# One order for the opening of a convolution module: squares on three engines, sums in pairs, the norm inside one product, loads by three queues

## The chip, the cores and the metric

The kernel runs on one core of a Trainium2 chip. The metric is the device time of one execution in microseconds. Five engines work side by side, each with its own stream of instructions: TensorE (PE in the profile) multiplies matrices into PSUM, VectorE (DVE), ScalarE (ACT) and GpSimd (POOL) do elementwise work, and SyncE (SP) issues most of the loads. ACT and POOL have queues for loads too.

## The reference

Two layers of a decoder trunk on one sequence of 512 positions and 1024 channels, in float32. Layer 0 mixes by a convolution module, layer 1 by sparse attention; after each comes a SwiGLU block. The part that matters here is the opening of layer 0:

```python
def rmsnorm(x, g):
    xf = x.astype(jnp.float32)
    y = xf * lax.rsqrt(jnp.mean(xf * xf, axis=-1, keepdims=True) + RMS_EPS)
    return (y * g.astype(jnp.float32)).astype(x.dtype)

def conformer_conv_module(h, w_in, b_in, w_dw, b_dw, ln_g, ln_b, w_out):
    a, g = jnp.split(h @ w_in + b_in, 2, axis=-1)
    u = a * jax.nn.sigmoid(g)
    u = lax.conv_general_dilated(u, w_dw[:, None, :], ..., feature_group_count=D_MODEL) + b_dw
    ... # layer norm over channels, silu
    return u @ w_out

h = rmsnorm(x, norm_mix[0]); x = x + conformer_conv_module(h, ...)
```

## The kernel before

Everything is kept transposed: channels on the 128 partitions, the 512 positions along the free dimension. `x` is eight tiles x0 to x7. Products are made at nearly float32 precision from halves: each operand is split into a rounded high part and the rest, its low part, and three matmuls (high by high, low by high, high by low) are added in PSUM. ACT writes the high parts, `wh` of a weight unit (L233) and `hh` of an x tile (L327, multiplied by the norm's gain). DVE writes the low parts, `wl` (L242) and `hl` (L328).

Weights come in units. Units 0 to 3 (`cw_s`, 256 KB) hold the columns of the first output tile, two x tiles' rows each. Units 4 to 17 (`cw_in`, 512 KB) hold one output tile each. SP loads them into three buffers `wr`; `wh` and `wl` have two buffers each.

The module's first product has 16 output tiles: A0 to A7 are the values and G0 to G7 the gates of eight groups of 128 channels. A0 and G0 are made in the opening: for each x tile six matmuls, 48 in all (`mm3`, L293 to L295). Then come A1 (unit 4), G1 (unit 5), A2 (unit 6), G2 (unit 7), A3 (unit 8), G3 (unit 9) and so on, 24 matmuls each, made by `proj_tile` (A1 and G1 at L409 to L411, the others at L293 to L295).

The RMS norm's divisor is applied behind the product. The sum of squares over channels starts in `sum_x`: ACT or DVE squares an x tile and DVE adds it into `acc`. `norm_a` (L350) lets TensorE sum `acc` over partitions, and DVE finds the reciprocal root in twelve small instructions. `norm_b` (L361) lets TensorE spread the root over the partitions, and ACT copies it to `R`. `norm_1` calls the one after half of A1, `norm_2` the other after half of G1. From then on `glu` can work: DVE multiplies the gate and the value by R, ACT takes the sigmoid, and DVE writes `u`. DVE then convolves some groups tap by tap (`cv`), POOL others from taps that ACT scales (`pv<-pv,tap`, L546), and TensorE the rest with band matrices (`cpe<-uf,bd`, L593), which POOL loads behind a copy of one column (`held`, L485).

A scheduler orders the instructions of each engine; `tc.keep_in_program_order` fixes the place of those it is called on.

Of the kernel before, what the change touches and what calls it, by code (L numbers as in the profile page):

```python
# [11 lines left out]
F32R = mybir.dt.float32r  # L12
BF16 = mybir.dt.bfloat16
I32 = mybir.dt.int32
AF = mybir.ActivationFunctionType
# [53 lines left out]
NPH = PH_B + 8 * len(PE_CONV)  # L69
WARM0 = 10  # L70
WARMS = {"t": 2, "r": 5}
SUM_V = (0, 3)


QV_ORDER = (0, 1, 2, 3, 4, 5, 6, 7, 8, 9)
# [59 lines left out]
def trunk(ctx: ExitStack, tc: tile.TileContext, A, out):  # L135
# [9 lines left out]
    def nm(s):  # L145
        cnt[0] += 1
        return f"{s}_{cnt[0]}"
# [67 lines left out]
    def parted(ins):  # L215
        return ins if hold[0] == "pe" else held(ins)

    def w_dma(i):
# [4 lines left out]
        raw_dma[i] = parted(after(nc.sync.dma_start(t[:, :cols], ap), state.get("behind")))  # L223
        raws[i] = t

    def w_hi(i):
# [31 lines left out]
    zb = cst.tile([P, P], BF16, name="zb")  # L258
    nc.vector.memset(zb, 0.0)
    dummy = cst.tile([P, 1], F32, name="dummy")  # L260
    nc.scalar.activation(dummy, zb[:, :1], AF.Copy)
    vec = cst.tile([P, NVEC], F32, name="vec")
    nc.sync.dma_start(vec, A["vec"])
    x = [xp.tile([P, T], F32, tag=f"x{m}", name=f"x{m}") for m in range(NK)]
    for m in range(NK):
        nc.sync.dma_start(x[m], A["xT"][m])
        if m in (0, 2, 4):
            w_dma(m // 2)
    cx0 = ExitStack()
    cb = cx0.enter_context(tc.tile_pool(name="cb", bufs=1, side="right"))  # L270
# [10 lines left out]
    def v(col, n=1):  # L281
        return vec[:, col:col + n]
# [37 lines left out]

    hh, hl = [None] * NK, [None] * NK

    def split_x(m, gcol):
        hh[m] = hps[0].tile([P, T], F32R, tag=f"hh{m}", name=nm(f"hh{m}"))
        hl[m] = hps[0].tile([P, T], F32R, tag=f"hl{m}", name=nm(f"hl{m}"))
        g = v(gcol + m)
        parted(nc.scalar.activation(hh[m], x[m], AF.Copy, scale=g))  # L327
        parted(nc.vector.scalar_tensor_tensor(hl[m], x[m], g, hh[m], ALU.mult, ALU.subtract))  # L328

    def sum_x(m, acc, eng=None, on_v=False):  # L330
        sq = acc if m == 0 else tp.tile([P, T], F32, tag="sq", name=nm("sq"))
        if on_v:
            nc.vector.tensor_tensor(sq, x[m], x[m], ALU.mult)
        else:
            parted(nc.scalar.activation(sq, x[m], AF.Square))
        if m > 0:
            parted((eng or nc.gpsimd).tensor_tensor(acc, acc, sq, ALU.add))

# [59 lines left out]
                    hooks[k]()  # L398
        return pss

    def proj_tile(pool, tag, xh=None, xl=None, mid=None, fixed=False):
        xh, xl = xh or hh, xl or hl
        ps = pool.tile([P, T], F32, tag=tag, name=nm("pp"))
        wh, wl = next_w()
        for k in range(NK):
            c = slice(k * P, (k + 1) * P)
            if fixed:
                kept = tc.keep_in_program_order
                kept(nc.tensor.matmul(ps, wh[:, c], xh[k], start=k == 0, stop=False))  # L409
                kept(nc.tensor.matmul(ps, wh[:, c], xl[k], start=False, stop=False))  # L410
                kept(nc.tensor.matmul(ps, wl[:, c], xh[k], start=False, stop=k == NK - 1))  # L411
            else:
                mm3(ps, wh[:, c], wl[:, c], xh[k], xl[k], k == 0, k == NK - 1)
            if k == 3:
                w_lo()
                if mid:
                    mid()
        return ps


# [23 lines left out]


    def conv_module():
        acc = new_acc()
        with ExitStack() as cx:
            cp = cx.enter_context(tc.tile_pool(name="cp", bufs=1, side="right"))
            ct = cx.enter_context(tc.tile_pool(name="ct", bufs=2, side="right"))  # L450
# [20 lines left out]


            pend = [pm.tile([P, T], F32, tag="pm", name=nm("pp")) for _ in range(2)]
            for k in range(NK):
                split_x(k, V_NM0)
                if k % 2 == 0:
                    wh, wl = next_w()
                if k == 0:
                    load_tables()
                for m in range(2):  # L480
                    c = slice(k % 2 * 256 + m * P, k % 2 * 256 + (m + 1) * P)
                    mm3(pend[m], wh[:, c], wl[:, c], hh[k], hl[k], k == 0, k == NK - 1)
                sum_x(k, acc, nc.vector, k in SUM_V)
            held = ct.tile([P, 1], F32, name="held", bufs=1)
            tc.keep_in_program_order(nc.gpsimd.tensor_copy(held, hl[NK - 1][:, :1]))  # L485
            for n in range(BAND_BUFS):
# [3 lines left out]

            def norm_1():
                last["r"] = norm_a(acc, pa, "pa")

            def glu(i, pA, pG):
                gr = ct.tile([P, T], F32, tag="A", bufs=3, name=f"gr{i}")
# [249 lines left out]
                        conv_pe(PE_CONV.index(c), c, ups[c])  # L745

            for i in range(1, NK):
                pA = proj_tile(pm, "pm", mid=norm_1 if i == 1 else None, fixed=i == 1)

                def gated():  # L750
                    glu(i - 1, *pend)
                    after_glu(i - 1)

                def norm_2():
                    nonlocal R
                    R = norm_b(last["r"], pa, "pa")
                    gated()
# [1595 lines left out]
```

## Time and profile before

| what | us |
| --- | --- |
| median of 3 runs | 1163.84 |
| lowest and highest | 1162.61, 1164.09 |
| profiled execution | 1163.65 |
| its span, first to last instruction | 1161.9 |
| PE busy | 1149.5 (99%) |
| DVE busy | 950.6 (82%) |
| ACT busy | 642.0 (55%) |
| POOL busy | 312.1 (27%) |

A row of the timeline gives the start in the span, the duration, the engine, the line, the operation, what is written and read, and how many instructions are merged; in brackets stands how long the engine was idle before and what ended that. A row of the windows gives the stretch, the busy time of PE, PE's weight loads, DVE, ACT and POOL, the TensorE clock that was granted, the share of the DMA engines that was busy, and GB/s. A row of the waits gives who waited for whom, for how long in total, how often, and the longest.

### The profile page before, as it was taken

The page shows a single profiled execution, that of the slowest core. Times are in us where ns is not written, and L with a number is a line of the kernel's source. Part 1 is how long each engine was busy: PE and PEld are TensorE (multiplying, and loading weights), DVE is VectorE, ACT ScalarE, POOL GpSimd, SP SyncE. Part 2 cuts the span into 40 slices and gives each one's busy share as a digit, 9 for nine tenths or more (in the row PEclk, how much of TensorE's full clock was granted, in tenths as well). Part 3 has the DMA queues.
Part 4 walks back from the last instruction along what each step waited for, and adds up shares of the span by engine and source line. Part 5 has one row for each costly group of instructions (what it writes and reads, how often), then busy time and mean ns, then how long its engine had stood idle before and what let it go on. Part 6 is the DMA issues. An engine that isn't in the chain of part 4 may idle for free.

```text
span 1161.9 us, 20767 instructions
## 1 busy us (share of the span) xinstructions
PE 1149.5 (99%) x7645; PEld 989.9 (85%) x7645; DVE 950.6 (82%) x1874; ACT 642.0 (55%) x1207; POOL 312.1 (27%) x406
## 2 busy tenths in 40 slices
PE   9999899999999999999999999999999999999998
PEld 6788688899999989998778877778889999998998
DVE  6999798999999878874465888865798999987876
ACT  5665555555555555454344688864355555554443
POOL 2699102011111101210124577860001111110120
PEclk9999999999999999999999999999999999999999
DMA  8633727377777768844455211134326777766892
GB/s 297 280 101 113 203 94 228 109 179 181 192 188 179 178 187 226 180 122 125 135 158 139 80 29 34 31 110 127 109 91 168 189 185 190 188 174 175 222 194 96
DMA packets 81141, 179.69 MB, mean 155 GB/s; under 512 B 29328, under 2 KB 30992, under 8 KB 80016
## 3 DMA queue, kind: packets, MB, share of 16 engines
q1 hardware_dynamic: 56896, 105.26, 28.7%
q0 software_dynamic: 24144, 73.12, 27.9%
q8 instruction: 60, 0.98, 0.3%
q14 instruction: 41, 0.34, 0.1%
HBM read 163.50 MB, written 4.75 MB: 145 GB/s over the span
## 4 chain that ended last, share of the span: by engine, by line
PE 94%; DVE 4%; ACT 1%; issue 1%; DMA 0%; SPq 0%; POOL 0%; ACTq 0%; DVEq 0%
PE st L1000 43%; PE pp L293 8%; PE pp L295 8%; PE pp L294 8%; PE O L2030 3%; PE T L1998 3%; PE st L294 2%; PE st L293 2%; PE st L295 2%; PE cpe L593 2%; PE S L1952 2%; PE pp L411 2%; PE pp L409 2%; PE pp L410 2%; PE pv L1818 1%; PE S L1953 1%
## 5 line engine op out<-in xcount | busy, mean ns | idle before, releaser
L1000 PE MATMUL st<-bo,sh 128*128 128x256 f32 (+1 forms) x1008 | 259.8, 333 | 0.0
L233 ACT ACTIVATE wh<-wr 128x1024 fp32r<-128x1024 f32 (+3 forms) x144 | 148.9, 1035 | 153.5 <-issue 48.3
L242 DVE TENSOR_TENSOR wl<-wr,wh 128x1024 fp32r<-128x1024 f32 (+3 forms) x144 | 176.6, 1226 | 52.4 <-ACT wh L233 48.6
L1000 PE MATMUL st<-bo,sl 128*128 128x256 f32 x720 | 203.3, 282 | 0.0
L1000 PEld LDWEIGHTS st<-bo,sh 128*128 128x128 f32 x1008 | 170.6, 189 | 20.1
L1000 PEld LDWEIGHTS st<-bo,sl 128*128 128x128 f32 x720 | 136.7, 190 | 0.1
L295 PE MATMUL pp<-hh,wl 128*128 128x512 f32 x304 | 120.2, 398 | 2.2 <-DVE wl L242 2.2
L293 PE MATMUL pp<-hh,wh 128*128 128x512 f32 x304 | 120.7, 400 | 0.5 <-ACT hh L327 0.2
L294 PE MATMUL pp<-hl,wh 128*128 128x512 f32 x304 | 119.7, 395 | 0.0
L986 DVE TENSOR_TENSOR sl<-S,sh 128x512 fp32r<-128x512 f32 x144 | 93.1, 687 | 16.9 <-ACT sh L985 16.6
L1000 PE MATMUL st<-bo,wh 128*128 128x256 f32 (+1 forms) x432 | 103.1, 316 | 0.0
L1000 PE MATMUL st<-oz,soh 128*128 128x256 f32 x512 | 88.0, 277 | 0.0
L961 POOL DMA_DIRECT2D S<-fw_x x36 | 21.1, 588 | 235.1 <-ACT c L1015 127.2
L985 ACT ACTIVATE sh<-S 128x512 fp32r<-128x512 f32 x144 | 82.2, 619 | 0.3
L1039 ACT ACTIVATE g<-g 128x512 f32<-128x512 f32 x36 | 22.8, 633 | 106.6 <-DVE g L1036 106.6
L1000 PE MATMUL st<-bo,wl 128*128 128x256 f32 x288 | 80.4, 279 | 0.0
L967 POOL DMA_DIRECT2D S<-fw_x x36 | 42.7, 1185 | 136.7 <-DMA S<-fw_x 131.5
L1000 PEld LDWEIGHTS st<-oz,soh 128*128 128x128 f32 x512 | 77.5, 188 | 0.4
L546 POOL TENSOR_TENSOR pv<-pv,tap 128x512 f32<-128x512 f32 x49 | 71.2, 1454 | 19.7 <-ACT tap L540 16.4
L1000 PEld LDWEIGHTS st<-bo,wh 128*128 128x128 f32 x432 | 70.8, 188 | 6.6
L1986 POOL TENSOR_SCALAR Pm<-Pm,rq,gates 128x512 f32<-128x512 f32 (+2 forms) x96 | 66.9, 708 | 32.6 <-DVE rq L1976 21.6
L1000 PE MATMUL st<-oz,sol 128*128 128x256 f32 x256 | 71.6, 280 | 0.2
(327 smaller groups left out, 2834.3 us busy)
## 6 DMA issues: line engine op xcount, KB each, us to landing
S<-fw_x POOLq DMA_DIRECT2D x72, 512.0 KB, 5.9
wr<-fw_in SPq DMA_DIRECT2D x44, 512.0 KB
So<-fw_q POOLq DMA_DIRECT2D x38, 512.0 KB, 7.6
wr<-fw_q SPq DMA_DIRECT2D x24, 512.0 KB
bd<-bands POOLq DMA_DIRECT2D x8, 1280.0 KB, 13.9
r<-fw_x SPq DMA_DIRECT2D x36, 256.0 KB
wr<-cw_in SPq DMA_DIRECT2D x14, 512.0 KB
wr<-fw_p SPq DMA_DIRECT2D x12, 512.0 KB
```

Source lines behind the costliest of these rows:

```text
L233: state["wh"] = parted(after(nc.scalar.activation(hi[:, :cols], raws[i][:, :cols], AF.Copy), pin.get(AF)))
L242: parted(after(nc.vector.tensor_tensor(lo[:, :cols], raws[i][:, :cols], hi[:, :cols], ALU.subtract), pin.get(ALU)))
L293: held(nc.tensor.matmul(ps, wh, xh, start=first, stop=False))
L294: held(nc.tensor.matmul(ps, wh, xl, start=False, stop=False))
L295: held(nc.tensor.matmul(ps, wl, xh, start=False, stop=last))
L546: last["pool"] = after(nc.gpsimd.tensor_tensor(dst, c, z, ALU.add), last.get("pool"))
L967: pe(nc.gpsimd.dma_start(S[n].rearrange("p (a b) -> p a b", a=2), fw_x(n)[:, None, 2 * T:].to_broadcast([P, 2, T]), accum_op=ALU.add))
L985: pe(nc.scalar.activation(h_[:, c], z, AF.Copy))
L986: pe(nc.vector.tensor_tensor(l_[:, c], z, h_[:, c], ALU.subtract))
L1000: nc.tensor.matmul(out, a[:, k], b, start=f, stop=z, skip_group_check=True))
L1986: kept(nc.gpsimd.tensor_scalar(Pt, Pt, sm[:, k:k + 1], gates[:, t + k, br * 16 + h:br * 16 + h + 1], ALU.mult, ALU.mult))
L1998: pe(nc.tensor.transpose(pt[:, c:c + P], rows(Us[par], t)[:, P * kc:P * kc + P], ident))
```

## The change

The opening is written out in one order. The loads are issued by three queues: `vec` (the gains) by POOL, unit 0 by ACT, the x tiles and the rest by SP. ACT's table load at the start is that of the sigmoid. For each pair of x tiles ACT makes `wh` and two `hh`, DVE `wl` and two `hl`, and TensorE takes all products with `hh` first and those with `hl` last. Squares go to DVE (x0, x3), ACT (x1, x2, x4, x6) and POOL (x5, x7), each into the tile `u` of its number, and are added in pairs by POOL (0+1, 0+2, 5+7) and DVE (3+4, 3+6, 3+0, 3+5); the sum ends in tile 3. The root follows the second x tile of A1, the spread the seventh (`ROOT_AT`); G1 has neither.

```diff
-SUM_V = (0, 3)
+ROOT_AT = (1, 6)
+ACC = 3
+def _start(nc, low):
+    v, a, p = nc.vector, nc.scalar, nc.gpsimd
+    return (
+        (lambda s, g: s(v, 0),),
+        (lambda s, g: s(a, 1), lambda s, g: g(p, 0, 1)),
+        (lambda s, g: s(a, 2), lambda s, g: s(p, 5), lambda s, g: s(v, 3)),
+        (lambda s, g: s(a, 4), lambda s, g: s(p, 7), lambda s, g: s(a, 6), lambda s, g: g(p, 0, 2)),
+        (lambda s, g: g(p, 5, 7), lambda s, g: g(v, 3, 4), lambda s, g: g(v, 3, 6), lambda s, g: g(v, 3, 0),
+         lambda s, g: low(4), lambda s, g: g(v, 3, 5)),
+    )
...
-    nc.scalar.activation(dummy, zb[:, :1], AF.Copy)
+    tc.keep_in_program_order(nc.scalar.activation(dummy, zb[:, :1], AF.Sigmoid))
-    nc.sync.dma_start(vec, A["vec"])
+    nc.gpsimd.dma_start(vec, A["vec"])
+    w_dma(0, nc.scalar)
     for m in range(NK):
         nc.sync.dma_start(x[m], A["xT"][m])
-        if m in (0, 2, 4):
+        if m in (2, 4):
             w_dma(m // 2)
...
-            for k in range(NK):
-                split_x(k, V_NM0)
-                if k % 2 == 0:
-                    wh, wl = next_w()
-                if k == 0:
+            def square(eng, k):
+                sqs[k] = vch[k]
+                if eng is nc.scalar:
+                    pe(nc.scalar.activation(vch[k], x[k], AF.Square))
+                else:
+                    pe(eng.tensor_tensor(vch[k], x[k], x[k], ALU.mult))
+            def gather(eng, a, b):
+                pe(eng.tensor_tensor(sqs[a], sqs[a], sqs[b], ALU.add))
+            for i in range(NK // 2):
+                w_hi(i)
+                split_hi(2 * i, V_NM0)
+                split_hi(2 * i + 1, V_NM0)
+                w_lo(i)
+                split_lo(2 * i, V_NM0)
+                split_lo(2 * i + 1, V_NM0)
+                for f in START[i]:
+                    f(square, gather)
+                state["next"] += 1
+                for k in range(i, i + 4):
+                    w_dma(k)
+                if i == 0:
                     load_tables()
-                for m in range(2):
-                    c = slice(k % 2 * 256 + m * P, k % 2 * 256 + (m + 1) * P)
-                    mm3(pend[m], wh[:, c], wl[:, c], hh[k], hl[k], k == 0, k == NK - 1)
-                sum_x(k, acc, nc.vector, k in SUM_V)
+                wh, wl = split[i]
+                for part in range(2):
+                    for k in (2 * i, 2 * i + 1):
+                        for w, z in ((((wh, hh), (wl, hh)), ((wh, hl),))[part]):
+                            for m in range(2):
+                                ...
+                                pe(nc.tensor.matmul(pend[m], w[:, c], z[k], ...))
+            w_hi(4)
+            for f in START[4]:
+                f(square, gather)
+            w_hi(5)
+            w_lo(5)
...
-                pA = proj_tile(pm, "pm", mid=norm_1 if i == 1 else None, fixed=i == 1)
+                def norms(k):
+                    if k == ROOT_AT[0]:
+                        norm_1()
+                    if k == ROOT_AT[1]:
+                        norm_2()
+                        gated()
+                pA = proj_tile(pm, "pm", each=norms if i == 1 else None, fixed=i == 1)
...
-                pG = proj_tile(pm, "pm", mid=norm_2 if i == 1 else None, fixed=i == 1)
+                pG = proj_tile(pm, "pm", fixed=i == 1)
```

The first place is DVE's order at the end of the opening. Before, from the low part of unit 3 to the low part of unit 5 (`wl_233`, `wl_265` and `wl_305` are units 3, 4 and 5):

```order
L328 SCALAR_TENSOR_TENSOR hl_27_279<-x_83,vec,hh_26_278 128x512
L242 TENSOR_TENSOR wl_233<-wr_170,wh_232 128x512
L337 TENSOR_TENSOR acc_114<-acc_114,sq_256 128x512
L242 TENSOR_TENSOR wl_265<-wr_203,wh_264 128x1024
L337 TENSOR_TENSOR acc_114<-acc_114,sq_275 128x512
L337 TENSOR_TENSOR acc_114<-acc_114,sq_288 128x512
L242 TENSOR_TENSOR wl_305<-wr_235,wh_304 128x1024
```

Now, with the same units as `wl_246`, `wl_276` and `wl_285`; `u_143` is the tile in which the sum ends, `u_140` and `u_145` are POOL's:

```order
L257 TENSOR_TENSOR wl_246<-wr_171,wh_245 128x512 [waits DMAHW3_49,Activation_49]
L345 SCALAR_TENSOR_TENSOR hl_19_253<-x_82,vec,hh_17_248 128x512 [waits DMAHW1_49,Activation_49]
L345 SCALAR_TENSOR_TENSOR hl_20_255<-x_83,vec,hh_18_250 128x512 [waits DMAHW2_49,Activation_49]
L506 TENSOR_TENSOR u_143<-u_143,u_144 128x512 [waits DVE_49,Activation_49]
L506 TENSOR_TENSOR u_143<-u_143,u_146 128x512 [waits DVE_49,Activation_49]
L506 TENSOR_TENSOR u_143<-u_143,u_140 128x512 [waits DVE_49,Pool_49]
L257 TENSOR_TENSOR wl_276<-wr_202,wh_275 128x1024 [waits DMAHW7_49,Activation_49]
L506 TENSOR_TENSOR u_143<-u_143,u_145 128x512 [waits DVE_49,Pool_49]
L257 TENSOR_TENSOR wl_285<-wr_231,wh_284 128x1024 [waits DMAHW0_49,Activation_49]
```

The low part of unit 4 stood behind one sum of DVE's own; now it stands behind three, and the last of them waits for POOL.

The second place is POOL's order in the opening. Before, behind the memsets:

```order
L485 CAST held<-hl_27_279 128x1 [waits DVE_49]
L469 DMA bd_293<-bands 128x2560 x2
L469 DMA bd_296<-bands 128x2560 x2
L469 DMA bd_299<-bands 128x2560 x2
L546 ISA
```

Now:

```order
L506 TENSOR_TENSOR u_140<-u_140,u_141 128x512 [waits DVE_49,Activation_49]
L503 TENSOR_TENSOR u_145<-x_81 128x512 [waits DMAHW0_49]
L503 TENSOR_TENSOR u_147<-x_83 128x512 [waits DMAHW2_49]
L506 TENSOR_TENSOR u_140<-u_140,u_142 128x512 [waits Activation_49,Pool_49]
L506 TENSOR_TENSOR u_145<-u_145,u_147 128x512 [waits Pool_49]
L538 CAST held<-hl_20_255 128x1 [waits DVE_49]
L488 DMA bd_290<-bands 128x2560 x2
```

Five elementwise instructions came in ahead of the copy and of the band loads.

The third place is TensorE's order in A1 (`ssq` is the norm's sum). Before, from the tenth matmul of A1:

```order
L409 MATMUL pp_302<-hh_14_214,wh_264 128x512
L410 MATMUL pp_302<-hl_15_215,wh_264 128x512
L411 MATMUL pp_302<-hh_14_214,wl_265 128x512
L350 MATMUL ssq_322<-ones_104,acc_114 128x1 x4
L409 MATMUL pp_302<-hh_17_227,wh_264 128x512
```

Now, from the first matmul of A1 (`wl_276` is the low part of unit 4):

```order
L427 MATMUL pp_299<-hh_5_161,wh_275 128x512 [waits Activation_49]
L428 MATMUL pp_299<-hl_7_166,wh_275 128x512
L429 MATMUL pp_299<-hh_5_161,wl_276 128x512 [waits DVE_49]
L427 MATMUL pp_299<-hh_6_163,wh_275 128x512
L428 MATMUL pp_299<-hl_8_168,wh_275 128x512
L429 MATMUL pp_299<-hh_6_163,wl_276 128x512
L368 MATMUL ssq_308<-ones_104,u_143 128x1 [waits DVE_49]
```

The third matmul of A1 waits for the low part of unit 4, and the norm's sum follows the sixth.

More of the change, by code (lines that the diff above doesn't have):

```diff
@@ L216, in parted, with w_dma @@
         return ins if hold[0] == "pe" else held(ins)
-    def w_dma(i):
+    def w_dma(i, eng=None):
         if i in raws or i >= len(units):
@@ L222, in w_dma @@
         t = wp.tile([P, 1024], F32, tag="wr", name=f"wr{i}")
-        raw_dma[i] = parted(after(nc.sync.dma_start(t[:, :cols], ap), state.get("behind")))
+        raw_dma[i] = parted(after((eng or nc.sync).dma_start(t[:, :cols], ap), state.get("behind")))
         raws[i] = t
@@ L321, in trunk, with split_hi, split_lo, sum_x @@
     hh, hl = [None] * NK, [None] * NK
-    def split_x(m, gcol):
[L324 to L330, printed above, removed]
+    def split_hi(m, gcol):
+        hh[m] = hps[0].tile([P, T], F32R, tag=f"hh{m}", name=nm(f"hh{m}"))
+        parted(nc.scalar.activation(hh[m], x[m], AF.Copy, scale=v(gcol + m)))
+    def split_lo(m, gcol):
+        hl[m] = hps[0].tile([P, T], F32R, tag=f"hl{m}", name=nm(f"hl{m}"))
+        parted(nc.vector.scalar_tensor_tensor(hl[m], x[m], v(gcol + m), hh[m], ALU.mult, ALU.subtract))
+    def split_x(m, gcol):
+        split_hi(m, gcol)
+        split_lo(m, gcol)
+    def sum_x(m, acc, eng=None):
         sq = acc if m == 0 else tp.tile([P, T], F32, tag="sq", name=nm("sq"))
[L332 to L335, printed above, removed]
+        parted(nc.scalar.activation(sq, x[m], AF.Square))
         if m > 0:
@@ L399, in proj_start, with proj_tile @@
         return pss
-    def proj_tile(pool, tag, xh=None, xl=None, mid=None, fixed=False):
+    def proj_tile(pool, tag, xh=None, xl=None, mid=None, fixed=False, each=None):
         xh, xl = xh or hh, xl or hl
@@ L417, in proj_tile @@
                     mid()
+            if each:
+                each(k)
         return ps
@@ L446, in conv_module @@
     def conv_module():
-        acc = new_acc()
         with ExitStack() as cx:
@@ L473, in conv_module @@
             pend = [pm.tile([P, T], F32, tag="pm", name=nm("pp")) for _ in range(2)]
-            for k in range(NK):
-                split_x(k, V_NM0)
-                if k % 2 == 0:
-                    wh, wl = next_w()
-                if k == 0:
-                    load_tables()
-                for m in range(2):
-                    c = slice(k % 2 * 256 + m * P, k % 2 * 256 + (m + 1) * P)
-                    mm3(pend[m], wh[:, c], wl[:, c], hh[k], hl[k], k == 0, k == NK - 1)
-                sum_x(k, acc, nc.vector, k in SUM_V)
+            pe = tc.keep_in_program_order
+            START = _start(nc, w_lo)
+            hold[0] = True
+            sqs = {}
+            def square(eng, k):
[19 more added lines that the diff above has]
+                if i == 0:
+                    load_tables()
+                wh, wl = split[i]
[3 more added lines that the diff above has]
+                            for m in range(2):
+                                c = slice(k % 2 * 256 + m * P, k % 2 * 256 + (m + 1) * P)
+                                pe(nc.tensor.matmul(pend[m], w[:, c], z[k], start=k == 0 and w is wh and part == 0,
+                                                    stop=k == NK - 1 and part == 1))
+            w_hi(4)
[3 more added lines that the diff above has]
+            w_lo(5)
+            hold[0] = False
+            acc = sqs[ACC]
             held = ct.tile([P, 1], F32, name="held", bufs=1)
@@ L492, in norm_1, with norm_2 @@
                 last["r"] = norm_a(acc, pa, "pa")
+            def norm_2():
+                nonlocal R
+                R = norm_b(last["r"], pa, "pa")
             def glu(i, pA, pG):
@@ L752, in gated @@
                     after_glu(i - 1)
[L754 to L757, printed above, removed]
+                def norms(k):
[5 more added lines that the diff above has]
+                pA = proj_tile(pm, "pm", each=norms if i == 1 else None, fixed=i == 1)
                 if i > 1:
```

## The prediction

> **What bounds the kernel now.** I read the page first, then TensorE's waits up to 60 us, then the timeline of the opening engine by engine, and last the places where DVE and POOL work at once.
>
> From the page:
>
> ```profile
> span 1161.9 us, 20767 instructions
> PE 94%; DVE 4%; ACT 1%; issue 1%; DMA 0%; SPq 0%; POOL 0%; ACTq 0%; DVEq 0%
> ```
>
> TensorE carries 94% of the chain that ended last. Everything here is therefore counted as time by which TensorE gets later or earlier. From the timeline of TensorE and ACT (start, duration, instruction):
>
> ```profile
> 4.79 0.63 ACT L233 ACTIVATE wh<-wr 128x512 fp32r<-128x512 f32 x1
> 5.47 0.83 PE L293 MATMUL pp<-hh,wh 128*128 128x512 f32 x2
> ...
> 18.76 0.39 PE L295 MATMUL pp<-hh,wl 128*128 128x512 f32 x1
> 18.98 0.39 PE L409 MATMUL pp<-hh,wh 128*128 128x512 f32 x1
> ...
> 19.45 0.40 PE L411 MATMUL pp<-hh,wl 128*128 128x512 f32 x1
> ...
> 20.38 0.39 PE L409 MATMUL pp<-hh,wh 128*128 128x512 f32 x1
> ...
> 31.92 0.39 PE L293 MATMUL pp<-hh,wh 128*128 128x512 f32 x1
> ```
>
> The opening's 48 matmuls run from 5.47 to 18.98. From 18.98 to 20.38 six take 1.40, so one costs 0.233, and 48 would need 11.2: TensorE loses 2.3 us. Then A1 and G1 run with the norm's small products among them, and A2 begins at 31.92. TensorE's next waits, and the chain there (the pieces between are DVE's taps):
>
> ```profile
> PE pp L295 <- DVE wl L242: 2.2, 2, 1.7
> ...
> 48.84 2.08 DVE wl L242
> 50.91 0.04 issue
> 50.96 0.50 PE pp L295
> ```
>
> In G3 the third matmul waits 1.7 us for the low half of unit 9, late on DVE. After that:
>
> ```profile
> 60.00:95.00 35.00, 35.00 (x151) 28.08 (x150) 34.11 (x41) 22.86 (x33) 33.45 (x23) 1.00 0.32 92
> ```
>
> TensorE has no gap in these 35 us, with DVE busy for 34.1 and POOL for 33.5. So the change can win the 2.3 us of the opening and the 1.7 us of G3, about 4 us, and no more unless the end of the module moves too.
>
> **The change, part by part.**
>
> *Loads and the first matmul.* The loads of `vec` (now POOL) and of unit 0 (now ACT) leave SP, so x0 is SP's first load. ACT's unit-0 split began at 4.79, behind its hh of x0; now it is first, and hh follows 0.52 later and takes 0.71 (the hh of the rows below). I put the loads at 4.3, between 4.8 as before and a 0.9 earlier issue; TensorE then starts at about 5.6 (ends 5.2 and 6.0). POOL's smallest loads in the list of DMA issues, as a bound for `vec`:
>
> ```profile
> w<-cw POOLq DMA_DIRECT2D x4, 16.0 KB, 2.0
> kb<-cpos POOLq DMA_DIRECT2D x4, 8.0 KB, 4.3
> ```
>
> Issued at about 0.7, `vec` lands between 2.7 and 5.0, against about 4.9 when hh wants it: nothing, at most 0.1. Of the loads that follow, x7 and unit 3 are the last two of eleven in SP's queue. From the windows (the last column is GB/s):
>
> ```profile
> 5.40:12.00 6.60, 5.64 (x20) 3.41 (x20) 5.33 (x10) 5.36 (x11) 0.00 (x0) 1.00 1.03 380
> ```
>
> At 380 GB/s one of 256 KB takes 0.69, so unit 3 is there by 4.3 + 11 x 0.69 = 11.9, or 13 if a load hangs by a microsecond; its pair is due on TensorE at 5.6 + 36 x 0.233 = 14.0. Hidden.
>
> *One order.* High-part products of a pair come first, low parts of x last, so a pair waits for ACT and has 8 matmuls (1.9 us) of cover for DVE. With TensorE fed throughout, the opening ends at 5.6 + 11.2 = 16.8 and A1's third matmul, the first to need the low half of unit 4, could run at 17.3 instead of 19.45. That is the gain as TensorE sees it: 2.1 us.
>
> *Squares and sums.* Instructions of DVE and ACT from 3 to 19.4 us, grouped (count, then busy, mean ns):
>
> ```profile
> L328 DVE SCALAR_TENSOR_TENSOR hl<-x,vec,hh 128x512 fp32r<-128x512 f32 x8 | 5.9, 747 | 1.4 <-ACT hh L327 1.3
> L337 DVE TENSOR_TENSOR acc<-acc,sq 128x512 f32<-128x512 f32 x6 | 4.1, 686 | 0.0
> L242 DVE TENSOR_TENSOR wl<-wr,wh 128x512 fp32r<-128x512 f32 x4 | 2.7, 687 | 0.0
> L327 ACT ACTIVATE hh<-x,vec 128x512 fp32r<-128x512 f32 x8 | 5.4, 712 | 3.0 <-DMA x<-xT 3.0
> ```
>
> DVE had 2 squares and 7 sums, now 2 and 4; ACT 6 squares, now 4; POOL none, now 2 squares and 3 sums. On paper DVE is relieved by three instructions. The question is whether POOL's five lie beside DVE's work. DVE and POOL, from the timeline:
>
> ```profile
> 15.62 0.75 DVE L328 SCALAR_TENSOR_TENSOR hl<-x,vec,hh 128x512 fp32r<-128x512 f32 x1
> 16.28 0.69 DVE L242 TENSOR_TENSOR wl<-wr,wh 128x512 fp32r<-128x512 f32 x1
> 16.43 2.92 POOL L485 COPY held<-hl 128x1 f32<-128x1 f32 x1 [14.61 <-DVE hl L328]
> 16.88 0.69 DVE L337 TENSOR_TENSOR acc<-acc,sq 128x512 f32<-128x512 f32 x1
> 17.48 1.22 DVE L242 TENSOR_TENSOR wl<-wr,wh 128x1024 fp32r<-128x1024 f32 x1
> 18.62 1.49 DVE L337 TENSOR_TENSOR acc<-acc,sq 128x512 f32<-128x512 f32 x2
> ...
> 40.20 1.60 DVE L242 TENSOR_TENSOR wl<-wr,wh 128x1024 fp32r<-128x1024 f32 x1
> 40.80 2.15 POOL L546 TENSOR_TENSOR pv<-pv,tap 128x512 f32<-128x512 f32 x1
> ...
> 48.54 1.29 POOL L546 TENSOR_TENSOR pv<-pv,tap 128x512 f32<-128x512 f32 x1
> 48.84 2.07 DVE L242 TENSOR_TENSOR wl<-wr,wh 128x1024 fp32r<-128x1024 f32 x1
> ...
> 104.41 0.75 DVE L515 SCALAR_TENSOR_TENSOR cv<-u,wdw,bs 128x512 f32<-128x512 f32 x1
> 104.75 1.56 POOL L546 TENSOR_TENSOR pv<-pv,tap 128x512 f32<-128x512 f32 x1 [0.26 <-ACT tap L540]
> ```
>
> They do not. POOL's sum at 48.54 ends at 49.83, and DVE's split, dispatched at 48.84, ends at 50.91, 1.08 after that. POOL's sum at 40.80 ends at 42.95, 1.15 after DVE's split ended at 41.80. The sum at 104.75 ends at 106.31, 1.15 after the DVE instruction ended at 105.16. Where DVE reads both operands from SBUF, one of the two works and the other stands, to within 0.02 us. POOL's one-element copy at 16.43 stood for 2.9 us through four such DVE instructions. The spacing of DVE's starts gives their price: hl 0.66, a 512-wide split or sum 0.60, a 1024-wide split 1.14. POOL's price is 1.15 to 1.29.
>
> Every DVE instruction of the new opening is of that kind. DVE's order puts the low half of unit 4 behind the sum that takes in POOL's second sum, and so behind four of POOL's five instructions. Work that cannot overlap, from DVE's first split at about 5.0: 8 hl 5.3, 4 splits 2.4, 2 squares 1.2, 3 sums 1.8, the split of unit 4 1.1, together 11.8; POOL's four 4.6 to 5.2. The split ends at 21.4 to 22.0 with no gap at all. TensorE stands at A1's third matmul from 17.3, for 4.1 to 4.7 us, and passes it 2.0 to 2.6 later than before. Four matmuls on (0.9) it wants the finished sum, behind POOL's fifth instruction and DVE's last sum (1.15 to 1.29 + 0.60): 0.8 to 1.0 more. Before, six matmuls of A1 were done at 20.38; now at 23.2 to 24.0: 2.8 to 3.6 later.
>
> The Trainium skill ("SBUF — State Buffer", section Who interferes with whom) says that a Vector instruction with two SBUF inputs contends with a GpSimd one that reads SBUF; by its order of issue POOL's copy would have gone second, where this trace lets it wait for four.
>
> *The clock.* TensorE's one long wait before, and windows around it (TensorE's busy us first; the clock is the column before the last two):
>
> ```profile
> PE cpe L593 <- issue: 2.4, 1, 2.4
> ...
> 115.00:118.30 3.30, 0.89 (x29) 0.75 (x25) 3.23 (x5) 1.24 (x2) 3.06 (x4) 1.00 1.03 372
> 118.40:121.70 3.30, 3.30 (x36) 1.54 (x34) 3.19 (x5) 0.00 (x0) 2.39 (x2) 0.50 1.08 363
> ```
>
> After 2.4 us without work the clock was 0.50 for over 3.3 us. A wait of over 4 us should bring the same; half of it falls beside the wait for the sum, so I charge 0.5 to 1.2. A2 then starts 3.3 to 4.8 late, at 35.2 to 36.7.
>
> *Root, spread, table.* The spread now follows the sum's products by fifteen matmuls (3.5 us) in A1, instead of half a tile later. Since these products come late, R is ready at about 29 to 31, not some 5 us before the 30 of these rows:
>
> ```profile
> 29.96 1.28 ACT L497 ACT_TABLE_LOAD   x1
> 29.97 0.69 DVE L496 TENSOR_TENSOR gr<-pp,Rb 128x512 f32<-128x512 f32 x1 [2.22 <-ACT Rb L364]
> ```
>
> The table load of 1.28 leaves the way to u0 (it goes to the start, in place of the one there). That gains nothing for TensorE: DVE does unit 6's split meanwhile (1.14), has u0 done near 33, and waits until G1 is ready at 35 or later.
>
> *What is given back.* Counted from A2's start, the second gate's product still waits for the end of G2. From there to unit 9's split DVE has one tap less (0.77): the split ends 0.77 to 1.65 earlier against TensorE (the end 1.65 is the whole G3 wait, reached if POOL's sums fall beside the taps). Given back: 0.8 to 1.65.
>
> *POOL's later work.* Its band loads now stand behind the five instructions:
>
> ```profile
> 19.30 3.34 POOL L469 DMA_DIRECT2D bd<-bands  x6
> ```
>
> They go out near 25, and their first reader comes after 95: hidden. POOL's taps start with u1, some 3 us later than before; its last band load and the 2.4 us wait at 115 move along. I charge nothing, ends -1 and +1.
>
> Sum: 3.3 to 4.8 less 0.8 to 1.65: 1.7 to 4.0 us later, middle 2.9. The profiled execution took 1163.65, 0.19 under the median of the runs: 1163.65 + 2.9 = 1166.55, as a median 1166.7; I say 1166.6.
>
> **Rivals.**
>
> *POOL fits beside DVE* (the other side). If the 512-wide instructions leave POOL the gaps it needs, unit 4's split is done by 17.3 (DVE alone ends it at 5.0 + 11.8 = 16.8), R comes over 5 us earlier, and both waits go: 2.1 + 1.7 = 3.8, at least 3: 1160 to 1161. It decides at 17.3: POOL's four must be done by 16. The three overlaps above speak against it.
>
> *Half of it*: the hl instructions, which no row of the opening shows against POOL, do not shut it out. Then 2 of POOL's 4.9 us fit beside the last four hl (2.6), the split ends near 16.8 + 2.9 = 19.7, and with the sum behind it A2 is 0.6 to 1.7 late. The clock stays, G3 gives back about as much: 1162.8 to 1164.8, no change. The row at 104.41, a two-input instruction of the same form, speaks against it.
>
> *Turns*: POOL gets in after each DVE instruction. The same work in total, but the wait splits over the last pair and A1, no piece is long, and the clock stays: the sum without its 0.5 to 1.2, 1165 to 1166.4. The copy at 16.43 speaks against it. The order of issue that the Trainium skill states in that section ("SBUF — State Buffer", Who interferes with whom) would give this.
>
> **How the numbers follow.** Stand-off with one long wait 0.50, turns 0.15, half 0.15, fits 0.20. 0.2% is 2.3 us, about what a measurement of this kernel tells from no change. The long wait (1165.5 to 1167.9) is over 1166.2 in three of four: 0.38; turns adds 0.04: slower 0.42. Fits gives 0.20 and half 0.03: faster 0.23. The rest, 0.35, is no change. The range leaves out the faster part of "fits" and takes half a microsecond more than the long wait's end, for the wait at 115: 1160.4 to 1168.4. The likeliest case's own range is 1165.5 to 1167.9.
>
> **What would show it.** TensorE's first opening matmul near 5.6 and no gap over 0.5 until 17; then one wait of 4 us at A1's third matmul for DVE's low half, with a clock of 0.5 behind it. POOL's first sum dispatched soon after ACT's square of x1 and lasting several us. The wait at G3 under 1 us. Wrong if POOL's five last 1.3 each and end before 17, or if A2 starts before 31.9.

## The result, and the profile after

| kernel | median us (lowest to highest, runs) | ratio to before, 95% interval |
| --- | --- | --- |
| before, beside it | 1163.88 (1162.61 to 1165.32, 6) | |
| after | 1170.22 (1168.16 to 1173.40, 6) | 1.0055 [1.0039, 1.0071] |

The change made the kernel slower by about 6 us, twice what was forecast and above the range. The profiled execution of the kernel after took 1168.16 and was the fastest of its six; it is 4.5 behind the profiled execution of before (1163.65). From the page of the kernel after:

```profile
span 1166.4 us, 20769 instructions
PE 89%; DVE 5%; POOL 2%; DMA 2%; issue 1%; ACT 1%; POOLq 0%; DVEq 0%; ACTq 0%
```

POOL and the DMA engines now have 2% each of the chain that ended last; before they had 0%. The timeline of TensorE shows how the opening runs now (the bracket is the wait ahead of an instruction):

```profile
6.35 0.74 PE L528 MATMUL pp<-hh,wh 128*128 128x512 f32 x2 [0.91 <-ACT hh L341]
...
18.29 0.73 PE L528 MATMUL pp<-hh,wl 128*128 128x512 f32 x2 [2.17 <-DVE wl L257]
...
22.95 0.50 PE L429 MATMUL pp<-hh,wl 128*128 128x512 f32 x1
...
35.55 0.39 PE L309 MATMUL pp<-hh,wh 128*128 128x512 f32 x1
```

The opening starts at 6.35 instead of 5.47. TensorE waits 2.17 us for unit 3's low half, in the last pair. A1's third matmul, which needs unit 4's low half, runs at 22.95 instead of 19.45, and A2 (the last row) starts at 35.55 instead of 31.92: 3.63 late. The waits of TensorE up to 140 us:

```profile
PE cpe L650 <- DMA uf<-swap: 3.1, 1, 3.1
PE pp L528 <- DVE wl L257: 2.2, 1, 2.2
PE pp L311 <- DVE wl L257: 1.1, 1, 1.1
```

The wait at G3 (third row) shrank from 1.7 to 1.1, so 0.6 was given back. The first row is new; it stands at the end of the module, at group 7. Now the cause in the opening, DVE's rows first and POOL's behind them:

```profile
10.22 1.76 DVE L257 TENSOR_TENSOR wl<-wr,wh 128x512 fp32r<-128x512 f32 x1
11.90 2.97 DVE L345 SCALAR_TENSOR_TENSOR hl<-x,vec,hh 128x512 fp32r<-128x512 f32 x2
14.79 1.78 DVE L503 TENSOR_TENSOR u<-x 128x512 f32<-128x512 f32 x1
16.49 1.75 DVE L257 TENSOR_TENSOR wl<-wr,wh 128x512 fp32r<-128x512 f32 x1
...
21.67 1.22 DVE L257 TENSOR_TENSOR wl<-wr,wh 128x1024 fp32r<-128x1024 f32 x1
...
9.75 1.68 POOL L506 TENSOR_TENSOR u<-u,u 128x512 f32<-128x512 f32 x1 [6.65 <-ACT u L501]
11.39 2.93 POOL L503 TENSOR_TENSOR u<-x 128x512 f32<-128x512 f32 x2
14.28 3.41 POOL L506 TENSOR_TENSOR u<-u,u 128x512 f32<-128x512 f32 x2
```

While POOL's five instructions run, from 9.75 to 17.69, each of DVE's takes 1.5 to 1.8 us where the same kinds took 0.69 to 0.75 before. They alternate: POOL, DVE, POOL, DVE, five of each in 8.5 us, from 9.75 to 18.24. That is what the stand-off of the prediction (while one works, the other stands) would give with turns. Unit 4's low half starts at 21.67.

At the end of the module TensorE multiplies group 7. It needs two transfers: the group's tile makes a trip through memory (`swap<-u`, then `uf<-swap`), and its band matrices are the last that POOL loads. The chain of before there and POOL's load, and then the chain of after:

```profile
115.49 2.41 issue
...
122.50 4.82 PE cpe L593 x160
```

```profile
108.99 1.10 POOL L469 DMA_DIRECT2D bd<-bands  x2
```

```profile
106.91 0.69 DVE u L605
...
111.22 2.90 DMA swap<-u
114.14 11.16 DMA uf<-swap
125.43 6.16 PE cpe L650 x160
...
139.51 0.50 PE pp L402
```

TensorE ahead of group 7, and POOL, in the kernel after:

```profile
105.46 13.98 PE L650 MATMUL cpe<-uf,bd 128*64 128x64 f32 x470
```

```profile
110.37 4.03 POOL L603 TENSOR_TENSOR pv<-pv,tap 128x512 f32<-128x512 f32 x3 [2.26 <-ACT tap L597]
114.33 1.10 POOL L488 DMA_DIRECT2D bd<-bands  x2
```

Before, the second half of the trip was issued at 109.12 and TensorE came to group 7 at 122.50, without a wait for it. Now it is issued at 114.14, 5.0 later, and lands at 125.30 with TensorE standing. Three of the 5.0 are the lateness of the opening, less what G3 gave back. Two are new: DVE's order now has group 2's sum of DVE's and POOL's parts (`u<-cv,pv`, the first row of the chain of after) ahead of the last group's gate, and it waits 1.16 for POOL. The late gate holds up ACT's next tap, POOL stands 2.26 for it, and POOL's last band load goes out at 114.33 instead of 108.99, 5.3 later.

TensorE itself is not late when it comes to group 7. Before, it stood 2.41 at 115.49, for nothing that the profile shows, and then worked at half clock. Now its 470 products run through without that stop, and it is ready at 122.31 (125.43 less the wait of 3.12). So the opening's lateness reaches group 7 by the late transfers and not by TensorE. The products of group 7 then take 6.16 instead of 4.82, because the clock is 0.50 from 124.90 to 128.30. The module's output product (last row of the chain) starts at 139.51; before at 135.24. These 4.27 are nearly all of the 4.5 between the two profiled executions.

### The profile page after: what moved, and what is told of

The parts are those of the page before. It is cut to its first block, busy times and chain, and to the rows that moved or that the text cites. A ratio compares the mean times of both kernels' runs of the same rounds, so it can differ in the third digit from the quotient of the medians.

```text
span 1166.4 us, 20769 instructions
## 1 busy us (share of the span) xinstructions
PE 1151.3 (99%) x7645; PEld 991.5 (85%) x7645; DVE 953.8 (82%) x1871; ACT 639.8 (55%) x1204; POOL 317.8 (27%) x412
## 4 chain that ended last, share of the span: by engine, by line
PE 89%; DVE 5%; POOL 2%; DMA 2%; issue 1%; ACT 1%; POOLq 0%; DVEq 0%; ACTq 0%
PE st L1059 43%; PE pp L309 7%; PE pp L311 6%; PE pp L310 6%; PE O L2089 3%; PE T L2057 3%; PE st L310 2%; PE st L309 2%; PE st L311 2%; PE S L2011 2%; PE pp L429 2%; PE pp L427 2%; PE pp L428 2%; PE pv L1877 1%; PE S L2012 1%
## 5 line engine op out<-in xcount | busy, mean ns | idle before, releaser
L309 PE MATMUL pp<-hh,wh 128*128 128x512 f32 x288 | 115.3, 400 | 0.1
L311 PE MATMUL pp<-hh,wl 128*128 128x512 f32 x288 | 113.8, 396 | 1.1 <-DVE wl L257 1.1
L310 PE MATMUL pp<-hl,wh 128*128 128x512 f32 x288 | 113.7, 395 | 0.0
L1026 POOL DMA_DIRECT2D S<-fw_x x36 | 42.6, 1184 | 138.7 <-DMA S<-fw_x 133.0
```

The costliest lines, as they stand in the source:

```text
L309: held(nc.tensor.matmul(ps, wh, xh, start=first, stop=False))
L310: held(nc.tensor.matmul(ps, wh, xl, start=False, stop=False))
L311: held(nc.tensor.matmul(ps, wl, xh, start=False, stop=last))
L1026: pe(nc.gpsimd.dma_start(S[n].rearrange("p (a b) -> p a b", a=2), fw_x(n)[:, None, 2 * T:].to_broadcast([P, 2, T]), accum_op=ALU.add))
```

## Experiments

**The kernel after once more.**

> The changed kernel once more, for a second profile of it. Its six times spread from 1168.2 to 1173.4, those of before from 1162.6 to 1165.3, and the profiled execution was the fastest. Theory 'stand-off': the opening is the same every time, A2 starts at 35.5, and what differs lies behind 115 us, where the last group's round trip through DRAM (3.1 us of waiting in the first profile) meets the band load; a slower execution shows a longer wait there. Rival: the opening itself varies (the loads, the clock), and A2 starts later than 36.5 in a slower execution.

1169.62. A2 at 35.24, the output product at 140.2; the wait for group 7's trip was 3.9. The opening repeats to 0.3, the end of the module does not.

**POOL's five replaced by memsets.** Each becomes three memsets of the same tile, which read nothing. The kernel leaves out the sum of squares by this.

```diff
+                elif eng is nc.gpsimd:
+                    for _ in range(3):
+                        pe(nc.gpsimd.memset(vch[k], 1.0))
```

> The five squares and sums of POOL are left out; in the place of each stand three fills of the same tile, which only write (the norm's divisor is not the reference's). All orders and waits stay. Theory 'stand-off' (POOL's reads of SBUF and DVE's two-input instructions shut each other out): DVE's splits and low parts fall back to 0.7 each, the low half of unit 4 is done by 18.5 instead of 22.9, A2 starts at 30.5 to 31.5 instead of 35.5, and the time falls by 4 to 6 us below the changed kernel's, to 1164 to 1166. Rival 'late feed' (the loads over POOL's queue and the late first matmul, 6.35 instead of 5.47, set the opening): A2 stays after 34 and the time within 1.5 us of the changed kernel's.

1164.47, ratio 1.0003 [0.9992, 1.0013]: 5.7 less than after. From the timeline of DVE, TensorE's start of A2, and the chain at the end of the module:

```profile
11.52 0.69 DVE L257 TENSOR_TENSOR wl<-wr,wh 128x512 fp32r<-128x512 f32 x1 [1.43 <-ACT wh L248]
12.13 1.41 DVE L345 SCALAR_TENSOR_TENSOR hl<-x,vec,hh 128x512 fp32r<-128x512 f32 x2
13.46 0.69 DVE L506 TENSOR_TENSOR u<-x 128x512 f32<-128x512 f32 x1
...
18.44 1.22 DVE L257 TENSOR_TENSOR wl<-wr,wh 128x1024 fp32r<-128x1024 f32 x1
...
32.29 0.40 PE L309 MATMUL pp<-hh,wh 128*128 128x512 f32 x1
...
110.80 11.10 DMA uf<-swap
...
122.03 6.43 PE cpe L657 x160
```

DVE's instructions are back at 0.69, unit 4's low half starts 3.2 earlier, A2 is at 32.29. With POOL busy from 8.22 to 16.42 but not reading, the stand-off is gone. It is shown. A2 is later than the theory's 30.5 to 31.5, because DVE now waits 1.43 for ACT (first row). The profiled execution took 1167.23, the longest of its eleven: group 2's sum still stands ahead of the last gate, the trip is issued 1.7 later than before, and TensorE, ready at 119.0, waits 3.0 for it and then works at half clock (last row).

**POOL's five done by ACT and DVE.**

```diff
-        ... s(p, 5) ... s(p, 7) ... g(p, 0, 1) ... g(p, 0, 2) ... g(p, 5, 7)
+        ... s(a, 5) ... s(a, 7) ... g(v, 0, 1) ... g(v, 0, 2) ... g(v, 5, 7)
```

> POOL's two squares go to ACT and its three sums to DVE, in the same places of the order. Theory 'stand-off': DVE has 13.6 us of its own before the low half of unit 4 is done and nobody shuts it out: done at 19 to 19.5, A2 at 31.5 to 32.5, about as before the change; time 1163 to 1166, as the end of the module falls. Rival 'DVE is simply too full': three more sums on DVE make it later still, A2 at 35.5 or more, and the time is 1170 or more.

1170.65, ratio 1.0053 [1.0039, 1.0067]. The opening ran at DVE's plain prices and A1 began at 17.4, but unit 4's low half still came after all of DVE's sums (A1's third matmul at 19.6, A2 at 33.7). Behind that the scheduler gave ACT and DVE another order, and TensorE waited 2.5 us for a unit's high half at 45. The low half is done at 19.6, as the theory had it to 0.1; the time is the rival's, and A2 lies between the two. So the time doesn't separate the theories.

**Group 2's sum behind the last gate.**

```diff
+                        if i == 2 and "gated" not in last:
+                            later.append(whole_sum)
...
             after_glu(NK - 1)
+            for z in later:
+                after(z(), last["glu"])
```

> The changed kernel with one instruction of DVE elsewhere: the sum of group 2's two parts, which waits for POOL, comes behind the gate of the last group instead of ahead of it. Theory 'end of module' (the last group's gate is late because it stands behind that sum, and its round trip through DRAM then collides with the band load): the last u is written near 107.5 instead of 111.2, the wait of 3.1 us at the last group's band product shrinks under 1.5, and the time falls by 1 to 3 us below the changed kernel's; the opening stays, A2 at 35.5. Rival (the band load alone sets the start of that product): the wait stays, and the time with it, within 0.7 us.

1167.81, ratio 1.0031 [1.0019, 1.0043]: 2.4 less than after, with intervals that just overlap and the same A2 (35.5). Its chain:

```profile
112.46 11.64 DMA uf<-swap
...
124.24 2.52 PE cpe L654 x79
```

The trip is issued 1.7 earlier, POOL's last band load 1.8 earlier (112.57), and group 7 starts 1.2 earlier, at full clock; the output product starts at 137.85. So the end of the module had a loss of its own. Which of the two transfers it was, this run doesn't tell, since the edit moves both.

**The late gate alone, in the kernel before.**

```diff
-                y = nc.vector.tensor_tensor(gr, pG, R, ALU.mult)
+                y = after(nc.vector.tensor_tensor(gr, pG, R, ALU.mult), last.get(("whole", 2)) if i == NK - 1 else None)
```

> The kernel before, with one edit: the last group's gate on DVE is placed behind the sum of group 2, as the kernel after has it. Theory (the late gate and the round trip of group 7 behind it cost by themselves, whatever the opening does): the gate at 105 to 106.5 instead of 102.55, group 7's products 1 to 2.5 later than 122.5, the time 1 to 2.5 above before, 1165 to 1166.4. Rival (the gate hurts only when the opening has made everything late; the kernel before has room there): the gate is late all the same, the end of the module and the time stay within 0.6 of before.

1163.79, ratio 0.9994 [0.9985, 1.0003]: nothing lost. DVE's rows, SP's issue of the trip's second half, and the chain:

```profile
103.91 0.68 DVE L548 TENSOR_TENSOR u<-cv,pv 128x512 f32<-128x512 f32 x1
104.50 0.68 DVE L496 TENSOR_TENSOR gr<-pp,Rb 128x512 f32<-128x512 f32 x1
...
110.80 0.53 SPq L568 DMA_DIRECT2D uf<-swap  x1
...
122.67 4.82 PE cpe L593 x160
```

The rival held. The gate is 1.95 late and the trip 1.7, and group 7 starts 0.17 later. In this profiled execution (1166.17, the longest of its eleven) the output product starts at 135.41, 0.17 later too. The second half of the trip takes 11 to 12 and TensorE comes at 122.5, so the kernel before has room of 1.4 to 2.4 there (an estimate from these rows). But that room isn't given by an early opening alone: with the memsets the trip is issued at the same 110.80, the opening is 0.4 late, and TensorE waits 3.0. The difference is that TensorE stands 2.42 at 115.67 here, as in the kernel before, and with the memsets it doesn't. POOL's band load is no test here: it goes out at 109.30, only 0.3 late.

**Memsets and the deferred sum together.**

> The kernel after with two edits at once: POOL's three-operand squares and sums of the opening replaced by three memsets each of the same tile (the root of the squares is then not the reference's), and the sum of group 2 on DVE placed behind the last group's gate. Theory (two separate losses that add: the stand-off, 4.5 to 5.7, and the late gate with the round trip of group 7 behind it, 2 to 2.4): A1's third matmul at 19.0 to 19.7, A2 at 31 to 32.3, the wait ahead of group 7's products under 2.2, the time 1161.3 to 1163.0. Rival (the late gate is only what the late opening makes of the module's end, and goes with it): the deferral adds nothing to the memsets alone, 1164.0 to 1165.0.

1162.94, ratio 0.9987 [0.9978, 0.9996]. The deferral still gains 1.5 on the memsets (the intervals just overlap), by which the trip goes out at 109.24 and TensorE no longer waits for it. The two losses add, less than in full (7.3 against 5.7 + 2.4). A1's third matmul (20.1) and A2 (32.7) are 0.4 later than the theory allowed.

**`vec` over SP's queue again.**

```diff
-    nc.gpsimd.dma_start(vec, A["vec"])
+    nc.sync.dma_start(vec, A["vec"])
```

> The kernel after, with the table vec loaded first on SyncE's queue instead of POOL's; the first weight unit stays on ScalarE's queue. Theory (the slow small load over POOL's queue held the first high half of x back): the first opening matmul starts at 5.2 to 5.7 instead of 6.0 to 6.35, A2 starts 0.4 to 0.8 earlier (34.6 to 35.1 against 35.2 to 35.55), the time falls by 0.4 to 0.9, to 1169.3 to 1169.8 by the median. Rival (the stand-off of DVE and POOL sets the opening's end, and it starts from loads of x that this edit doesn't move): the first matmul comes earlier all the same, A1's third matmul stays at 22.7 to 22.95, A2 at 35.2 to 35.55, the time at 1170.2 within 0.3.

1168.53, ratio 1.0035 [1.0023, 1.0046]: 1.7 less than after, with intervals that overlap. The time line is the rival's, though: the opening starts at 5.30, a whole microsecond earlier, and A1's third matmul stands at 22.65:

```profile
5.30 0.87 PE L528 MATMUL pp<-hh,wh 128*128 128x512 f32 x2
```

A2 is at 35.2. Most of what the time gained isn't in the opening; in its one profile the output product starts at 137.5, behind a wait of 2.4 for POOL's band load and without a stretch at half clock. Whether the load does that is not settled.

**`vec` over POOL's queue, in the kernel before.**

> The kernel before, with the table vec loaded over POOL's queue instead of first on SyncE's. Theory (a small load costs more over POOL's queue than the place it frees on SyncE's): the first opening matmul at 6.0 to 6.4 instead of 5.5, A2 0.4 to 0.9 later than 31.9, the time 0.4 to 1.0 above before. Rival (TensorE's opening has slack, the later start is made up by the first weight-low and x-low waits): A2 within 0.2 of 31.9, the time within 0.4 of before.

1164.47, ratio 1.0001 [0.9992, 1.0010]. TensorE:

```profile
6.43 0.72 PE L293 MATMUL pp<-hh,wh 128*128 128x512 f32 x2 [1.37 <-ACT hh L327]
...
31.58 0.39 PE L293 MATMUL pp<-hh,wh 128*128 128x512 f32 x1
```

It starts 0.96 late and is at A2 0.34 early: the old opening's 2.3 us of slack swallow it.

**Both edits that helped, POOL kept.**

> The kernel after with both edits that helped it alone: vec first on SyncE's queue, and the sum of group 2 behind the last gate. POOL's squares and sums stay. Theory (separate losses, 1.7 and 2.4, that add): 1165.7 to 1166.7, A2 still at 35, no stretch at half clock up to 130. Rival (both edits mend the same end of the module, so the gains don't add): 1167.3 to 1168.2.

1167.81, ratio 1.0028 [1.0018, 1.0039]: as the deferral alone, so the gains do not add. In its profile (1169.81, the longest of its eight) the clock fell in A1, behind the waits:

```profile
23.60:30.40 6.80, 6.80 (x20) 5.54 (x20) 2.30 (x13) 0.00 (x0) 0.00 (x0) 0.50 1.01 422
```

A1's third matmul was at 22.3, A2 at 38.0, 15.7 later instead of 12.6: such a double stretch costs 3.1.

**Dummy products in the opening's waits.**

```diff
+                for _ in range(8 if i == 3 else 0):
+                    pe(nc.tensor.matmul(filler..., zb, zb..., start=True, stop=True))
```

> The kernel after with eight dummy products of zeros ahead of the fourth pair of the opening and four behind it, in the time in which TensorE waits for the low halves there. The planner now also puts the sum of group 2 behind the last gate's products on DVE, so it is to be compared with the version that defers that sum (1167.8). Theory (the waits of the opening cost more than their own length, since the granted clock falls to half behind them in some executions): no stretch at 0.5 in the opening, A2 at 35.0 to 35.6, the median 0.7 to 2 below 1167.8. Rival (the half-clock stretch lies in time that TensorE waits anyway): within 0.6 of 1167.8.

The dummies change DVE's later order too: the sum of group 2 stands behind the last gate, so this is compared with the deferral. 1166.33, ratio 1.0019 [1.0009, 1.0029]: 1.5 less, with intervals that overlap. TensorE's windows of this kernel, and of after:

```profile
18.00:22.60 4.60, 4.38 (x20) 2.80 (x18) 4.39 (x7) 1.06 (x1) 3.24 (x7) 1.00 0.70 187
```

```profile
19.10:22.50 3.40, 3.40 (x9) 2.64 (x8) 3.19 (x5) 0.17 (x1) 2.87 (x6) 0.50 0.82 227
```

The clock no longer falls in the opening, and A2 is at 35.26, where it is without the filling. The deferral's own execution has no half-clock stretch either, and its A2 is at 35.5. So a stretch that ends by 22.6 lies in time that TensorE waits anyway: the rival holds for the opening, although the time fell as the theory had it. The 1.5 seem to come later: this kernel's other order on DVE has no wait at G3.

**Three more executions of the kernel after.**

> The kernel after, unchanged, for one more time line. Theory (the median lies 2 above the first profiled execution because of what differs from one execution to the next: half-clock stretches in A1 and the slower pace of the products behind the module): A2 between 35.2 and 38.2, later where a half-clock stretch falls behind A1's third product; output product's start between 139.5 and 143; the rest behind it 1023.7 to 1026. Rival (the first profile is typical in all of these): A2 within 35.2 to 35.6, product's start within 139.5 to 140.2, the rest 1023.5 to 1024.5, and the time 1168 to 1169.6 each time.

> The kernel after, unchanged, once more: as the look before this one, by both theories.

> The kernel after, unchanged, a third time: as the two looks before this one, by both theories.

1170.96, 1168.21, 1169.23. A2 at 35.38, 35.40, 35.54; the output product at 141.86, 137.76 and 138.7; the rest behind it, to the end of TensorE's last matmul, 1024.2, 1025.5, 1025.6. The wait at the end of the module, in the first, the second and the third:

```profile
PE cpe L650 <- DMA bd<-bands: 2.8, 1, 2.8
```

```profile
PE cpe L650 <- DVE uf L654: 2.3, 1, 2.3
```

```profile
PE cpe L650 <- DMA bd<-bands: 3.1, 1, 3.1
```

The opening is fixed, as the rival had it; the module's end differs by 4 us, as the theory had it. What ends the wait differs as well: group 7's trip in two of the five executions, POOL's band load in two, and in one DVE's `uf<-cpe`, which stands behind another sum that waits for POOL. The executions with a half-clock stretch at 125 to 134 are at 139.5, 140.2 and 141.9, those without at 137.8 and 138.7.

**A version without POOL that does the whole computation.** One order, `vec` on SP, squares 0 and 3 on DVE and the others on ACT, all sums on DVE, six of them behind the low half of unit 4, the deferred sum, 11 warm-up products, the sum's products behind A1's fourth group of three.

> A version of the whole computation: the one order of TensorE and the first weight unit on ScalarE's queue as after; vec first on SyncE's queue; squares 0 and 3 on DVE and six on ScalarE, all sums on DVE and most of them behind the low half of unit 4, POOL none; the sum's products behind A1's fourth product group, the spread after A1; group 2's sum behind the last gate; 11 warm-up products instead of 10. Theory (no stand-off without POOL, the one order's gain of some 2 us stays): first matmul 5.2 to 5.7, A1's third at 16.8 to 18.0, A2 at 29.8 to 31.0, that is 1 to 2 ahead of the kernel before, the time 1160.0 to 1162.5. Rival (DVE, with the five operations of POOL added to it at 0.6 to 0.7 each, 3.2 in all, is itself the bound of the opening): the low half of unit 4 or the sum is late, a wait of 1.5 to 3 at A1, A2 at 32 to 33.5, the time 1163.5 to 1165.5.

1164.07, ratio 1.0000 [0.9991, 1.0008]. TensorE:

```profile
17.41 0.50 PE L430 MATMUL pp<-hh,wl 128*128 128x512 f32 x1
```

```profile
PE ssq L369 <- DVE u L507: 1.9, 1, 1.9
```

A1's third matmul is at 17.41, 2.04 before its 19.45: the gain of the one order is real. The wait for the sum (second row) takes 1.9 of it, and A2 is at 32.15, no earlier than before: the rival, with DVE as the bound, held. The same with the sum's products one group earlier:

> As the version with the sum's products behind A1's fourth product group, but with them behind its third, and the spread behind its seventh; DVE's later order puts the low half of each unit two taps earlier in groups 1 and 2. Theory: TensorE waits 0.5 to 1.2 for the sum there, and less than that at the later low halves; the time within 0.8 of the other version. Rival (the low halves' place in DVE's order decides): 1.5 to 2.5 less than the other version, whose TensorE then shows waits for wl of over 1 us between 31 and 56.

1166.11, ratio 1.0014 [1.0003, 1.0024]. It is 2.0 slower in the medians, as neither theory had it: the wait for the sum is 2.6 and the clock halves behind it (A2 at 34.9); no later wait for a low half is over 0.3 in either version. The first of the two once more:

> The version of the whole computation without POOL once more, unchanged, to tell its own time line from the pace of the products behind it. Theory (its opening and product end are fixed, only the pace of the long products later, 113 or 118 ns each, differs from one execution to the next): A2 at 31.8 to 32.5, the output product's start at 132.6 to 133.9, the time 1161.5 to 1165.5. Rival (its earlier start at the output product is itself an accident of one execution): the output product's start at 134.5 or later.

1164.64; A2 at 33.5 with a half-clock stretch at 23.2, the output product at 134.6 instead of 133.2. The output product lies in the rival's bounds: how early this version gets there is in part an accident of the execution. No version tried that does all the work is faster than before.

## Why the prediction was right or wrong

**Loads and the first matmul: too early.** Forecast 5.6 (ends 5.2 and 6.0), measured 6.35, and 6.0 to 6.4 in the other executions. `vec` over POOL's queue was to land between 2.7 and 5.0 and to cost 0.1 at most. It was issued later than the 0.7 assumed and took the longer of the two times quoted:

```profile
1.27 4.28 DMA vec<-vec
```

It landed at 5.55, behind the split of unit 0, which was itself no earlier than before (4.77). That cost little by itself: A1's third matmul moved 0.3 without it.

**One order: right.** The 2.1 us stand in the version without POOL, where A1's third matmul comes 2.04 earlier. The 11.2 for 48 matmuls stand in the run whose squares and sums ACT and DVE do: 6.12 to 17.38.

**The stand-off: right in kind and size, wrong in form.** DVE and POOL did exclude each other. But POOL got in after each DVE instruction, as the rival "turns" had it, given 0.15. This agrees with the Trainium skill ("SBUF — State Buffer", section Who interferes with whom), by which the order of issue decides who blocks. All five of POOL's instructions, and not four, so came ahead of unit 4's split, and the wait is split: 2.17 in the last pair, and behind it half-clock products until that low half is done at 22.89 (at full clock, in the deferral's execution, it shows as waits of 1.1 and 1.6). That rival took an unbroken clock and ended at 1166.4, so it doesn't give the time either. The sum's products start at 23.97, within the forecast's 23.2 to 24.0, and A2 at 35.55, within its 35.2 to 36.7. The copy at 16.43, which I held against it, was one instruction; from it nothing followed for a queue of five. In the kernel after the same copy takes 0.59, at 19.63, beside three sums of DVE.

**The clock: right that it falls, wrong that it costs there.** It fell to 0.50 from 19.10 to 22.50 although no single wait was over 2.2. With dummy products in the waits it stayed at 1.00 and A2 moved by 0.3 at most. The 0.5 to 1.2 charged were nil here. A2 still fell into the forecast's range, by luck: the stand-off alone made 3.6, the top of its 2.8 to 3.6, with DVE's first split at 5.44 instead of the 5.0 assumed.

**What is given back:** 0.6, under the 0.8 to 1.65. Up to here the sum holds, with one term at nothing and one under its range. Where the band matrices follow the last gate's product, in the timelines of before and of after, TensorE is 3.0 behind, against the forecast's middle of 2.9:

```profile
102.44 0.98 PE L593 MATMUL cpe<-uf,bd 128*64 128x64 f32 x26
```

```profile
105.46 1.15 PE L650 MATMUL cpe<-uf,bd 128*64 128x64 f32 x32
```

**POOL's later work and the end of the module: the step that failed.** It was charged nothing, with ends of -1 and +1, since "its last band load and the 2.4 us wait at 115 move along". The band load moved by 5.3 instead of 3. The wait at 115 did not move along: it is gone in all five executions of after, and TensorE's 3.0 with it. So the forecast's 2.9, which was right at 105, is not the loss that was measured. That loss is a new wait at group 7, of 3.1 in the profiled execution, and 1.3 of slower products behind it.

Three of the 5.0 by which the trip is late come from the opening, two from the sum of group 2 that DVE's order put ahead of the last gate. The forecast looks at DVE's new order only in the opening, and it has no term for the room that group 7's transfers have. Over five executions the output product is 2.5 to 6.6 later than in the profile of before, 4.4 on average, against the 2.9 forecast. Without the stand-off (memsets) the time falls by 5.7, without the late gate by 2.4, without both by 7.3, against a loss of 6.3: the two together make up the change's loss.

**What stays open.** The five profiled executions of after average 1169.2, some 5 above the medians of before; the first six runs had a median 6.3 above. The rest behind the output product is no different between the kernels (1023.5 to 1025.9 in all). So about 1 us of the medians' distance is in no profile. Why TensorE stands 2.4 us at 115 in the kernel before and not after is not shown. No run moves the trip and POOL's band load apart, so their shares are open.

## What to carry to other kernels

Work given to an idle POOL isn't free beside a DVE that reads two operands from SBUF: look for rows in which one of them takes twice its time while the other works, before moving anything there. A delay is followed to the next transfers behind it, and their room (when they land, when their reader comes) is a term of the sum; a wait that stands in the profile before need not move along with the rest. Where a scheduler sets the order, the whole order is compared, also hundreds of instructions behind the edit.

## What the runs showed of the hardware

The pace of the FFN's products isn't fixed: in the same stretch, at a granted clock of 1.00 and without a gap, one execution does more products than another. Windows of before, and of the second of the three more executions of after:

```profile
480.00:516.00 36.00, 36.00 (x293) 34.84 (x292) 30.95 (x49) 21.22 (x28) 3.67 (x10) 1.00 0.52 132
```

```profile
480.00:516.00 36.00, 36.00 (x284) 34.92 (x283) 30.87 (x49) 21.00 (x27) 4.70 (x8) 1.00 0.53 127
```

There the products follow each other at about 113 or at about 118 ns for over a hundred in a row. It makes up to 2.4 us between two executions (1023.5 to 1025.9 behind the output product), whatever the opening does.

The clock fell to 0.50 in stretches of 3.4 us, in the opening of all five executions of after behind waits of 1.0 to 2.2 us; with the deferral, or with `vec` on SP, the one profiled execution has none there, with waits of 1.1 and 1.6. The Trainium skill ("TensorE: Matmul & The Clock Gate", Part 1: The HAM clock gate) has a free-running window of that length, after one idle one of which the clock is halved; the length agrees, but a whole idle window wasn't needed here.
